# x^T's two parts at the front of their pool, laid out as k-tile, token tile, token

## The chip, the cores and the metric

The program runs on one core of a Trainium2 chip. Its time is the time on the device in microseconds (us). The kernel before took 1495.61 us, the median of three runs that went from 1495.11 to 1495.95.

## The reference

The reference is two transformer-like blocks on one sequence of 256 tokens with 1024 features, all in float32. The first is an FFN, a mixer (a causal convolution beside chunked gated linear attention), a second FFN and a gated projection. The second has two layers; each is an FFN, a mixing step (differential attention in the first layer, spatial gating in the second) and another FFN, and each part is scaled, shifted and gated by vectors made from a condition. Cut to what matters here:

```python
def _swiglu(x, w_in, w_out):
    gate, up = jnp.split(x @ w_in, 2, axis=-1)
    return (jax.nn.silu(gate) * up) @ w_out

def first_block(x, p, ...):
    h = x
    h = h + 0.5 * _swiglu(_rmsnorm(h, ffn1_norm), ffn1_w_in, ffn1_w_out)
    z = _rmsnorm(h, mix_norm) @ w_in            # convolution and linear attention from z
    h = h + jnp.concatenate([y_conv, y_gla], axis=-1) @ w_out
    h = h + 0.5 * _swiglu(_rmsnorm(h, ffn2_norm), ffn2_w_in, ffn2_w_out)
    gate = jax.nn.sigmoid(_rmsnorm(h, ple_norm) @ ple_w_gate)
    h = h + gate * (p @ ple_w_proj)
    return _rmsnorm(h, final_norm)

def second_block(x, c, ...):
    for i in range(2):
        h = modulate(rms_norm(x, ln_ffn1[i]), sh1, sc1)
        x = x + 0.5 * g1 * swiglu(h, ffn1_wg[i], ffn1_wu[i], ffn1_wd[i])
        h = modulate(rms_norm(x, ln_mix[i]), sh2, sc2)
        x = x + g2 * mix(h)                     # attention, then spatial gating
        h = modulate(rms_norm(x, ln_ffn2[i]), sh3, sc3)
        x = x + 0.5 * g3 * swiglu(h, ffn2_wg[i], ffn2_wu[i], ffn2_wd[i])
        x = rms_norm(x, ln_out[i])
    return x
```

Every `@` with a large weight multiplies the normalized activations of all 256 tokens by a weight of 1024 (or 2816) rows.

## The kernel before, in words

The 256 tokens are two token tiles of 128. Before each projection, `norm_T` normalizes a tile, transposes it on TensorE (line 571) and stores x^T, features on the partitions, in eight k-tiles of 128 features.

Float32 products are made from float32r parts: a value is a high part H and a low part L, and a product is three products, H·H, L·H and H·L. So x^T is held as `xh` and `xl` (lines 377 and 378, written by ScalarE's cast and VectorE's subtraction in `split`, lines 498 and 499), and each weight as `wh` and `wl` (lines 196 and 197). The weights come as a stream of 318 entries of 1 MB, three in flight, each split when there is room.

x^T is used in two ways. In `chunk`, with `mm3` (lines 490 to 492), 128 tokens of x^T for one k-tile are the weights that TensorE loads, and 512 columns of `wh` or `wl` are streamed. In `chunkT`, with `mmT` (line 692), 128 columns of `wh` or `wl` are loaded, and x^T of all 256 tokens for one k-tile is streamed: with the token tile as the outer index in `xh`, this is two pieces of 128 elements. An FFN takes its first two of eleven gate and up chunks by `chunk`, the other nine by `chunkT`; each of the nine is 8 k-tiles x 4 column blocks x 3 products = 96 products of line 692. Between two chunks come the down projection's products with `g` (128 tokens of the activated product, high and low) as weights, again by `mm3`. The other tiles whose names end in `HL` (`cHL` of the convolution, `oHL` of the attention) are weights of `mm3` too, and `wglr` is a small weight that line 692 loads in the mixer (tile `glr`).

The order of work is set by the program's order and by a scheduler with priorities; generators interleave the norms of one token tile with the products of the other. The pool `const` holds `h`, `kc`, `cols`, `neghalf`, `ones_r`, `xh`, `xl`, `cact` in the order in which `setup` asks for them, each rounded up to a multiple of 32 bytes in each partition.

Of the kernel before, what the change touches and what calls it, by code (L numbers as in the profile page):

```python
# [30 lines left out]
# buffers of each tag; tiles of one tag are handed out in the order of the program,  # L31
# so chains of work that run beside each other have tags of their own
# [6 lines left out]
# how many down-projection steps a tile does alone at the end of an FFN,  # L39
# and how many gate/up chunks the first tile does alone at its start  # L40
TAIL = 3
HEAD = 2
# taps of the convolution issued per us of the tensor engine's work
CONV_RATE = 3.0
# taps of each channel that the tensor engine takes
# [4 lines left out]
# how far ahead of its place in the program the scheduler may take a chain's work  # L50
# [6 lines left out]
# ---------------------------------------------------------------- weights  # L57
# Each entry of the stream is [128, 2048]: two blocks [128, 1024] of a weight.
#   "c": four k-tiles x 512 columns (two of each 1 MB entry make 8 k-tiles)
#   "d": two k-tiles x 1024 columns  # L60
#   "ada": transposed, two blocks of 128 columns of a modulation vector x 1024 rows
# [33 lines left out]
# the modulation vectors of the second block (shift, scale, gate of each part)  # L95
# are made while these FFNs run: layer, vectors
# [30 lines left out]
# columns of the packed per-partition constants  # L127
# [17 lines left out]
# columns of the shape-only constants  # L145
K_ID, K_LOW, K_UP, K_END, K_CAUSAL = 0, 128, 256, 384, 384
# rows
# [3 lines left out]
class Stream:  # L151
    """The weights, in order: DMA ahead, then split into H + L, float32r parts
    whose sum is the float32 weight."""
# [21 lines left out]
    def pump(self, now=False, n=0):  # L175
        """splits what there is room for, or n halves of an entry"""
# [38 lines left out]
class Task:  # L215
    """A chain of work given as a generator. What it yields is how much work of the
    tensor engine (us) is to be issued before the chain goes on, or a task to wait for."""
# [7 lines left out]
class Kernel:  # L225
# [25 lines left out]
    # -------------------------------------------------------------- order of issue  # L251
    @contextmanager
    def ahead(self, n):
        """the scheduler takes what is traced inside as if it were n instructions earlier"""
        tc = self.tc
        at = tc.cur_priority
        tc.cur_priority = at - n
        yield
        tc.cur_priority += n

    def pin(self, i):
        """what `after` is given later does not go before i on its engine"""
        self.pins[i.ins.engine] = i.ins
# [8 lines left out]
    def hold(self, on):  # L272
        """no weights are split while a chain runs that the tensor engine waits for"""
        self.held = on
        if not on:
            self.ws.pump()
# [31 lines left out]
    def tick(self, us):  # L308
        """so much work of the tensor engine has been issued"""
# [22 lines left out]
    # -------------------------------------------------------------- tiles  # L332
# [11 lines left out]
    def junk(self):  # L344
        """what only its sum is needed of"""
        return self.sp.tile([P, 512], BF16, tag="junk", name=self.nm("junk"), bufs=1)
# [7 lines left out]
    def psa(self, s, i, shape):  # L354
        """a bank of the accumulators, where none is in use"""
        return self.pacc.tile(shape, F32, tag=f"acc{i // 2}{i % 2}", name=self.nm(s))
# [10 lines left out]
    # -------------------------------------------------------------- start  # L367
    def setup(self):
        nc, a = self.nc, self.a
        self.h = [self.cpool.tile([P, D], F32, name=f"h{t}") for t in range(NT)]  # L370
# [4 lines left out]
        self.ones_r = self.cpool.tile([P, P], F32R, name="ones_r")  # L375
        nc.gpsimd.memset(self.ones_r.bitcast(F32), 1.0)
        self.xh = self.cpool.tile([P, NT, KT, P], F32R, name="xh")
        self.xl = self.cpool.tile([P, NT, KT, P], F32R, name="xl")
# [3 lines left out]
        # the first function of the scalar engine, of the table that the others here are in too  # L382
# [12 lines left out]
    def start(self):  # L395
        """x^T of the input, and the first weights"""
# [17 lines left out]
        # products of ones, that nothing reads, bring the tensor engine to its full clock  # L414
# [20 lines left out]
    # -------------------------------------------------------------- modulation  # L435
# [18 lines left out]
    def ada_end(self, layer, v, s):  # L454
        """a modulation vector: in columns, the gates in rows"""
# [30 lines left out]
    # -------------------------------------------------------------- pieces  # L486
# [8 lines left out]
    def split(self, dst, src):  # L495
        """dst = (H, L), src float32 in SBUF or PSUM"""
# [10 lines left out]
    def square(self, x, s):  # L507
        """sum of squares / 1024 of half a row"""
# [4 lines left out]
    def rstd(self, ss, t):  # L513
        """1/rms from the two halves' sums; with four, also that of 1/rms times what the other two are of"""
# [6 lines left out]
        if n == 2:  # L521
            # (s2 / (s1 + eps) + eps)^-1/2 (s1 + eps)^-1/2 = (s2 + eps (s1 + eps))^-1/2
# [6 lines left out]
    def residual(self, t, hf, gate, scale, keep):  # L529
        """h + gate * acc, half a row: in h, or keeps h"""  # L530
# [16 lines left out]
    def norm_T(self, t, ss, a, b=None):  # L547
        """x^T of tile t: (h / rms) * a + b, features on partitions, as H and L"""
# [40 lines left out]
        for hf in range(2):  # L589
            sl = slice(4 * hf, 4 * hf + 4)  # L590
            for i in self.split((self.xh[:, t, sl, :], self.xl[:, t, sl, :]), xas[hf]):
                if self.held:
                    self.pin(i)
            yield 0.5
# [5 lines left out]
    def xk(self, t, k):  # L600
        return self.xh[:, t, k, :], self.xl[:, t, k, :]
# [9 lines left out]
    def finish(self, t, scale=None, gate=None, a=None, b=None, row=None, upd=None, last=False):  # L611
        """h += ..., then the norms that lead to the next x^T"""
# [38 lines left out]
    # -------------------------------------------------------------- projections  # L651
    def chunk(self, key, t, ps):
        """ps[128 tokens, 512] = x @ chunk, over 8 k-tiles"""
# [8 lines left out]
    def by_tile(self, name, cs, pss=None):  # L662
        """several chunks, all of them for one token tile before the next"""
# [6 lines left out]
    def chunkT(self, key, banks):  # L670
        """the transpose of x @ chunk: 128 columns on the partitions, all tokens;
        bank [128, 2, 256] i of the two has column blocks i and i + 2"""
# [3 lines left out]
        for k in range(KT):  # L676
            h, l = self.ws.get((*key, k // 4), (k % 4) // 2)
            for cb in range(4):
# [3 lines left out]
                    (self.xh[:, :, k, :], self.xl[:, :, k, :]), k == 0 and cb < 2, k == KT - 1,  # L682
# [4 lines left out]
    def mmT(self, out, w, x, first, last):  # L687
        """out[columns, tokens] += w^T x; the groups of a bank share its first start"""
# [8 lines left out]
    def down(self, t, units, first, last):  # L697
        """acc[t] += x[k-tile]^T @ weight[k-tile] over units (key, half, x)"""
# [10 lines left out]
    def down2(self, name, order, xs, fin):  # L709
        """the product with a weight of four entries: the first token tile ends early enough  # L710
        for its norms to run beside the rest of the second's"""
# [14 lines left out]
    def ffn(self, name, fin):  # L726
# [39 lines left out]
        # first chunks: a token tile at a time, so that the first need not wait for the second  # L766
# [25 lines left out]
    # -------------------------------------------------------------- first block: mixer  # L792
    def mixer_load(self):
        nc, a = self.nc, self.a
        yield 30.0
        # the 16 columns of the gate's low rank, padded to the array's width
# [15 lines left out]
    def conv_taps(self, b):  # L812
        """depthwise causal convolution of a block of channels, a tap at a time"""
# [16 lines left out]
    def conv_diag(self):  # L830
        """diagonal matrices of the last taps, for each block of channels"""
# [9 lines left out]
    def conv_pe(self, bs):  # L841
        """the last taps of some blocks of channels, as products with diagonal matrices"""
# [41 lines left out]
    def gla_gates(self, zt):  # L884
        """decays of the gated linear attention, channels on the partitions"""
# [42 lines left out]
    def gla_scores(self, banks, gates):  # L928
        """q, k with their decays; scores inside the chunks of 64; k of the chunks' end by tokens"""
# [17 lines left out]
        for t in range(NT):  # L947
# [6 lines left out]
            for e in range(2):  # L954
                # a bank for each half of the array's rows
# [12 lines left out]
    def gla_state(self, c):  # L968
        """S_{c+1} = exp(cum_end) * S_c + k_end^T v"""
# [77 lines left out]
    def mixer(self, fin):  # L1047
# [4 lines left out]
        # a * sigmoid(b): the first half of the channels a token tile at a time  # L1052
# [33 lines left out]
        # low rank of the gates  # L1086
        pz = self.psg("glr", [P, S])
        for k in range(KT):
            self.mmT(
                pz, (self.wglr[0][:, k, :], self.wglr[1][:, k, :]), (self.xh[:, :, k, :], self.xl[:, :, k, :]),  # L1090
# [52 lines left out]
    # -------------------------------------------------------------- first block: per-layer embedding  # L1143
# [37 lines left out]
    # -------------------------------------------------------------- differential attention  # L1181
    def attn_load(self):
        """bias of each head by distance, and lambda"""
# [21 lines left out]
        # lambda_init + e0 - e1, negated  # L1205
# [8 lines left out]
    def attn_qk(self, c, t, ps):  # L1214
        """q or k of four heads: rms norm of the groups of 64, channels on the partitions"""
# [22 lines left out]
    def attn_softmax(self, hf, pr, t, lane):  # L1238
        """p0 - lambda * p1 of two heads, transposed"""
# [22 lines left out]
        for i in range(2):  # L1262
            # the bias is stored from the last key to the first
# [40 lines left out]
    def attn_values(self, hf, t, deps):  # L1304
# [12 lines left out]
        # squares scaled by 2^-40; a sum beyond float32's range gives 1/rms = 0  # L1317
# [62 lines left out]
    # -------------------------------------------------------------- spatial gating  # L1380
# [84 lines left out]
    # -------------------------------------------------------------- all of it  # L1465
# [57 lines left out]
# ---------------------------------------------------------------- host: layout only  # L1523
# [6 lines left out]
def pack(inputs):  # L1530
# [21 lines left out]
    def ch(dst, parts, half):  # L1552
        # parts: column blocks of a [1024, n] weight; four k-tiles of it
# [75 lines left out]
    # bucket of the distance n - 127  # L1629
# [38 lines left out]
```

## Time and profile before

| | |
|---|---|
| median of 3 runs | 1495.61 us (1495.11 to 1495.95) |
| span of the profiled execution | 1494.0 us |
| TensorE products (PE) | 1467.5 us busy, 98% |
| TensorE weight loads (PEld) | 1300.4 us, 87% |
| VectorE (DVE) | 1086.6 us, 73% |
| ScalarE (ACT) | 782.3 us, 52% |
| DMA | 232 GB/s in the mean |

The time of the profiled execution is given by its span, 1494.0 us from the first to the last instruction; the median of the runs is 1.6 us more, which lies around the span. Products on TensorE overlap: the record of a product is longer than the distance to the next one's start, so the duration in a row is no pace. A pace is the distance between two starts, or the length of a stretch divided by its products.

### The profile page before, as it was taken

The numbers are of one execution on the slowest core, as the hardware profiler recorded it, in microseconds if no ns is written. First come the engines' busy times: TensorE is split into PE (matmuls) and PEld (weight loads), VectorE is DVE, ScalarE is ACT, GpSimd is POOL, SyncE is SP. The second block draws the span as 40 slices with busy tenths as digits, with TensorE's granted clock in tenths as the row PEclk, the third lists the DMA queues.
The fourth block names the chain that finished last, engine by engine and source line by source line (L and its number), as shares of the span: only waits on it lengthen the run. The fifth ranks groups of instructions, "written<-read, shape, count | busy, mean of one in ns | idle before, by whom it ended". The sixth has DMA issues, their size and how long they took to land.

```text
span 1494.0 us, 23272 instructions
## 1 busy us (share of the span) xinstructions
PE 1467.5 (98%) x9256; PEld 1300.4 (87%) x9256; DVE 1086.6 (73%) x1693; ACT 782.3 (52%) x1238; POOL 55.2 (4%) x60
## 2 busy tenths in 40 slices
PE   8999999999999999999999999999999999999998
PEld 6999989779999878999776889998899988889997
DVE  6876569978775688775678788866987658685554
ACT  6544566265444584444586554446544455554442
POOL 1000000100000000000122100000000000000000
PEclk9999999999999999999999999999999999999999
DMA  8887544138776448786445388863899846276550
GB/s 311 335 310 267 191 149 183 64 134 319 296 290 233 148 157 320 301 315 216 155 141 199 116 330 347 325 249 127 312 350 335 300 145 235 105 291 225 205 204 29
DMA packets 52332, 346.06 MB, mean 232 GB/s; under 512 B 5912, under 2 KB 8704, under 8 KB 11776
## 3 DMA queue, kind: packets, MB, share of 16 engines
q1 hardware_dynamic: 52224, 344.58, 62.2%
q8 instruction: 72, 1.18, 0.3%
q14 instruction: 36, 0.29, 0.1%
HBM read 343.47 MB, written 1.09 MB: 231 GB/s over the span
## 4 chain that ended last, share of the span: by engine, by line
PE 80%; DVE 9%; ACT 4%; DMA 3%; issue 2%; POOL 2%; SPq 0%; POOLq 0%; DVEq 0%; ACTq 0%
PE gu L692 39%; PE acc L492 9%; PE acc L490 9%; PE acc L491 9%; DVE wl L197 4%; DMA raw<-wpack 3%; PE gu L491 2%; PE gu L492 2%; PE gu L490 2%; ACT wh L196 1%; DVE cacc L824 1%; PE xT L571 1%; POOL rn L504 1%; ACT s L1275 1%; PE cv L848 1%
## 5 line engine op out<-in xcount | busy, mean ns | idle before, releaser
L197 DVE TENSOR_TENSOR wl<-raw,wh 128x1024 fp32r<-128x1024 f32 x490 | 588.2, 1221 | 244.2 <-ACT wh L196 243.4
L196 ACT CAST wh<-raw 128x1024 fp32r<-128x1024 f32 x490 | 502.2, 1050 | 396.4 <-DMA raw<-wpack 159.4
L692 PE MATMUL gu<-xh,wh 128*128 128x256 f32 x1728 | 484.3, 281 | 1.8 <-DVE g L736 1.1
L692 PE MATMUL gu<-xl,wh 128*128 128x256 f32 x1728 | 482.2, 279 | 0.0
L692 PE MATMUL gu<-xh,wl 128*128 128x256 f32 x1728 | 482.1, 279 | 0.0
L692 PEld LDWEIGHTS gu<-xh,wh 128*128 128x128 f32 x1728 | 324.8, 188 | 5.1 <-DVE g L736 1.7
L692 PEld LDWEIGHTS gu<-xl,wh 128*128 128x128 f32 x1728 | 324.8, 188 | 2.4
L692 PEld LDWEIGHTS gu<-xh,wl 128*128 128x128 f32 x1728 | 324.8, 188 | 0.0
L492 PE MATMUL acc<-wl,g 128*128 128x512 f32 x528 | 207.2, 392 | 0.0
L490 PE MATMUL acc<-wh,g 128*128 128x512 f32 x528 | 207.2, 394 | 0.0
L491 PE MATMUL acc<-wh,g 128*128 128x512 f32 x528 | 206.5, 391 | 0.0
L447 DVE SCALAR_TENSOR_TENSOR raw<-raw,cact 128x1024 f32<-128x1024 f32 x144 | 171.7, 1219 | 17.9 <-DMA raw<-wpack 17.8
L492 PEld LDWEIGHTS acc<-wl,g 128*128 128x128 f32 x528 | 99.1, 188 | 22.4
L491 PEld LDWEIGHTS acc<-wh,g 128*128 128x128 f32 x528 | 99.1, 188 | 20.8 <-DVE g L499 1.2
L490 PEld LDWEIGHTS acc<-wh,g 128*128 128x128 f32 x528 | 99.2, 188 | 18.8
L734 ACT ACTIVATE s<-gu 128x256 f32<-128x256 f32 x108 | 40.7, 384 | 78.5 <-PE gu L692 78.3
L490 PE MATMUL gu<-wh,xh 128*128 128x512 f32 x192 | 76.7, 400 | 1.8 <-ACT wh L196 1.4
L492 PE MATMUL gu<-wl,xh 128*128 128x512 f32 x192 | 76.1, 398 | 1.4 <-DVE wl L197 1.4
L491 PE MATMUL gu<-wh,xl 128*128 128x512 f32 x192 | 76.3, 398 | 0.5 <-DVE xl L499 0.5
L736 DVE TENSOR_TENSOR g<-gu,s 128x256 f32<-128x256 f32 x108 | 44.6, 420 | 30.1 <-ACT s L734 29.5
L504 POOL TENSOR_TENSOR rn<-nv,neghalf 128x1 f32<-128x1 f32 (+1 forms) x22 | 20.1, 912 | 1244.6 <-DVE nv L518 1025.8
L498 ACT CAST g<-g 128x256 fp32r<-128x256 f32 x108 | 43.3, 407 | 38.1 <-DVE g L736 37.3
(308 smaller groups left out, 1623.6 us busy)
## 6 DMA issues: line engine op xcount, KB each, us to landing
raw<-wpack SPq DMA_DIRECT2D x316, 1024.0 KB, 4.9
gate<-grow SPq DMA_DIRECT2D x6, 512.0 KB, 4.2
row<-rows SPq DMA_DIRECT2D x5, 512.0 KB, 5.7
bias<-fd SPq DMA_DIRECT2D x16, 128.0 KB, 4.1
raw<-wpack SPq DMA_DIRECT2D x2, 512.0 KB, 7.1
out<-h SPq DMA_DIRECT2D x4, 256.0 KB, 2.2
h<-x SPq DMA_DIRECT2D x2, 256.0 KB
h<-x SPq DMA_DIRECT2D x1, 512.0 KB
```

The source lines that it names most:

```text
L196: self.last = k.after(nc.scalar.copy(out=h, in_=raw[:, u, :]))
L197: k.after(nc.vector.tensor_sub(out=l, in0=raw[:, u, :], in1=h.bitcast(F32)))
L447: self.after(nc.vector.scalar_tensor_tensor(out=raw[:, u, :], in0=raw[:, u, :], scalar=1.0, in1=self.cact, op0=ALU.mult, op1=ALU.mult, acc ...
L490: nc.tensor.matmul(out, lhsT=xh, rhs=wh, start=first, stop=False)
L491: nc.tensor.matmul(out, lhsT=xl, rhs=wh, start=False, stop=False)
L492: nc.tensor.matmul(out, lhsT=xh, rhs=wl, start=False, stop=last)
L498: self.nc.scalar.copy(out=dst[0], in_=src),
L504: self.nc.gpsimd.tensor_tensor(out=r, in0=v, in1=self.neghalf[:, :n], op=ALU.pow)
L571: self.last_T = nc.tensor.transpose(ps[:, i, :], xn[hf][:, i * P : (i + 1) * P], self.ident)
L692: nc.tensor.matmul(out, lhsT=ww, rhs=xx, start=first and n == 0, stop=last and n == 2, skip_group_check=True)
L734: nc.scalar.activation(s, b[:, 0, :], AF.Silu)
L736: nc.vector.tensor_mul(out=y, in0=b[:, 1, :], in1=s)
```

## The change

`xh`, `xl` and `ones_r` are asked for first in their pool, and the two parts of x^T change their layout from [token tile, k-tile, token] to [k-tile, token tile, token]. All that reads or writes them indexes accordingly. The rest of the difference between the two files is removed comments, which move later line numbers by one at most (line 692 becomes 693, lines 490 to 492 become 491 to 493).

```diff
     def setup(self):
         nc, a = self.nc, self.a
+
+        self.xh = self.cpool.tile([P, KT, NT, P], F32R, name="xh")
+        self.xl = self.cpool.tile([P, KT, NT, P], F32R, name="xl")
+        self.ones_r = self.cpool.tile([P, P], F32R, name="ones_r")
         self.h = [self.cpool.tile([P, D], F32, name=f"h{t}") for t in range(NT)]
...
-        self.ones_r = self.cpool.tile([P, P], F32R, name="ones_r")
         nc.gpsimd.memset(self.ones_r.bitcast(F32), 1.0)
-        self.xh = self.cpool.tile([P, NT, KT, P], F32R, name="xh")
-        self.xl = self.cpool.tile([P, NT, KT, P], F32R, name="xl")
...
-            for i in self.split((self.xh[:, t, sl, :], self.xl[:, t, sl, :]), xas[hf]):
+            for i in self.split((self.xh[:, sl, t, :], self.xl[:, sl, t, :]), xas[hf]):
...
     def xk(self, t, k):
-        return self.xh[:, t, k, :], self.xl[:, t, k, :]
+        return self.xh[:, k, t, :], self.xl[:, k, t, :]
...
-                    (self.xh[:, :, k, :], self.xl[:, :, k, :]), k == 0 and cb < 2, k == KT - 1,
+                    (self.xh[:, k, :, :], self.xl[:, k, :, :]), k == 0 and cb < 2, k == KT - 1,
...
-                pz, (self.wglr[0][:, k, :], self.wglr[1][:, k, :]), (self.xh[:, :, k, :], self.xl[:, :, k, :]),
+                pz, (self.wglr[0][:, k, :], self.wglr[1][:, k, :]), (self.xh[:, k, :, :], self.xl[:, k, :, :]),
```

In the built programs this gives the following addresses (byte in each partition, and what is left over 128):

| tile | before | after |
|---|---|---|
| `xh` | 118432 (32) | 106624 (0) |
| `xl` | 126624 (32) | 114816 (0) |
| `ones_r` | 117920 (32) | 123008 (0) |
| `wh`, `wl` | 41088 and on (0) | same |
| `g`, `oHL` | 169536 and on (64) | same |
| `wglr` | 185920, 206400 (64) | same |
| `cHL` | 139520 and on (0) | same |

`h`, `kc`, `cols` and `neghalf` move too, and each keeps its remainder, 0. The slices that a product takes of any of these tiles start at a multiple of 512 bytes from the tile's start. Streamed x^T of one k-tile was two pieces of 512 bytes, 4096 bytes apart, and is one of 1024 bytes; a write of half a k range of one token tile was one piece of 2048 bytes, and is four of 512 bytes, 1024 bytes apart. No instruction is added, removed or moved on any engine, and each waits for what it waited for.

## Rows read from the trace of the kernel before

**Rows 1.** The page: busy us of each engine, and clock by slices.

```profile
PE 1467.5 (98%) x9256; PEld 1300.4 (87%) x9256; DVE 1086.6 (73%) x1693; ACT 782.3 (52%) x1238; POOL 55.2 (4%) x60
PEclk9999999999999999999999999999999999999999
```

**Rows 2.** Chain that ended last: start us, us, what.

```profile
4.02 9.93 DMA raw<-wpack
22.55 7.44 DMA raw<-wpack
44.62 6.44 DMA raw<-wpack
72.28 11.21 PE gu L692 x96
...
462.32 11.20 PE gu L692 x96
...
1458.86 11.21 PE gu L692 x96
```

**Rows 3.** Timeline, first and last of 94: start us, us, engine line op.

```profile
1232.96 0.40 PE L492 MATMUL si<-wl,xh 128*128 128x512 f32 x1
...
1254.66 0.39 PE L492 MATMUL su<-wl,xh 128*128 128x512 f32 x1
```

**Rows 4.** Timeline, g as weights, first and last of 39.

```profile
493.61 0.39 PE L492 MATMUL acc<-wl,g 128*128 128x512 f32 x1
...
502.32 0.39 PE L492 MATMUL acc<-wl,g 128*128 128x512 f32 x1
```

**Rows 5.** Timeline, cHL as weights, first and last of 39.

```profile
307.94 0.39 PE L492 MATMUL acc<-wl,cHL 128*128 128x512 f32 x1
...
316.77 0.39 PE L492 MATMUL acc<-wl,cHL 128*128 128x512 f32 x1
```

**Rows 6.** Timeline, wglr as weights, first and last of 24.

```profile
225.31 0.28 PE L692 MATMUL glr<-xh,wglr 128*128 128x256 f32 x1
...
228.06 0.28 PE L692 MATMUL glr<-xh,wglr 128*128 128x256 f32 x1
```

**Rows 7.** Groups by form: line, names, xcount, busy us, mean ns, idle before.

```profile
L692 PE MATMUL gu<-xh,wh 128*128 128x256 f32 x1728 | 484.3, 281 | 1.8 <-DVE g L736 1.1 <-DVE g L775 0.7
L492 PE MATMUL acc<-wl,g 128*128 128x512 f32 x528 | 207.2, 392 | 0.0
L490 PE MATMUL gu<-wh,xh 128*128 128x512 f32 x192 | 76.7, 400 | 1.8 <-ACT wh L196 1.4 <-ACT xh L498 0.3
```

**Rows 8.** Timeline, 128-wide products in a row.

```profile
196.12 1.04 PE L571 MATMUL xT<-kc,xn 128*128 128x128 f32 x8
...
823.92 2.84 PE L1314 MATMUL o<-v,aT 128*128 128x128 f32 x24
```

**Rows 9.** Groups by form: the writes of x^T, and 128-wide operations.

```profile
L499 DVE TENSOR_TENSOR xl<-xa,xh 128x512 fp32r<-128x512 f32 x40 | 25.9, 685 | 5.7 <-ACT xh L498 5.7
L498 ACT CAST xh<-xa 128x512 fp32r<-128x512 f32 x40 | 23.3, 637 | 0.0
L580 ACT ACTIVATE xa<-xT,mod,mod 128x128 f32<-128x128 f32 x48 | 18.0, 456 | 4.7 <-PE xT L571 4.7
L584 DVE TENSOR_SCALAR xa<-xT,mod,mod 128x128 f32<-128x128 f32 x48 | 16.3, 402 | 0.2 <-PE xT L571 0.2
```

**Rows 10.** Waits of TensorE: us in total, times, longest.

```profile
PE gu L491 <- DVE xl L499: 0.5, 1, 0.5
PE gu L490 <- ACT xh L498: 0.3, 1, 0.3
```

**Rows 11.** Timeline, products (PE) and weight loads (PEld) side by side.

```profile
72.47 0.28 PE L692 MATMUL gu<-xh,wh 128*128 128x256 f32 x1
72.47 0.19 PEld L692 LDWEIGHTS gu<-xl,wh 128*128 128x128 f32 x1
72.59 0.28 PE L692 MATMUL gu<-xl,wh 128*128 128x256 f32 x1
```

## The prediction

> **What bounds the kernel now.** [...] Busy time of overlapping products hides their pace, so next I took the chain of waits. After the first 57 us, which hang on weight transfers and splits, it runs through block after block of 96 products of line 692 in 11.20 to 11.21 us [rows 2], with nothing between them. Start to start that is 11.21 / 96 = 116.8 ns. Everything that this change can give or cost lies in such paces: how far apart TensorE starts two neighbouring products. The built program has the same instructions in the same order on every engine, with the same waits, so nothing is issued earlier or later by rule; only where x^T lies and how it is stepped through is new.
>
> The third view is the timeline, for the pace of 512-wide products by what their weights are. With x^T as weights, 94 starts take 1254.66 - 1232.96 = 21.70 us, 233.3 ns each [rows 3]. With g as weights, 39 starts take 8.71 us, 229.2 ns [rows 4]. Both stream the same wh and wl (on multiples of 128 bytes), both at full clock, with no wait between. What differs is the address: g starts 64 past a multiple of 128, x^T 32 past one. A third kind, cHL, lies on a multiple of 128 and takes 8.83 us for 39 starts, 232.4 ns [rows 5]. So the pace does depend on address, by 1 to 4 ns. For 256-wide products there is one such pair: with wh or wl as weights (multiples of 128) 116.8 ns, with wglr (64 past) 24 starts in 2.75 us, 119.6 ns [rows 6], while the streamed x^T is the same.
>
> **The change part by part.**
>
> *x^T as weights, 512 wide.* The heads of the six FFNs have 192 such products on each of lines 490, 491 and 492 [rows 7], 576 in all; counted from the code, qkv, v, ab, r, si, su and the last product of the first block add 192, 144, 48, 48, 96, 96 and 96: 1296. Their address goes from 32 past a multiple of 64 to a multiple of 128. The ends are g's pace and cHL's: 233.3 - 229.2 = 4.1 ns gives -5.3 us, 233.3 - 232.4 = 0.9 ns gives -1.2 us. cHL is the nearer by address, g by far the better sampled (528 products per line, [rows 7]). I take the middle, 2.5 ns: -3.2 us. No 512-wide row in this trace is steadily slower than 233.3, so I put no loss here.
>
> *x^T streamed, 256 wide.* Line 692 has 1728 products of each of three kinds for gate and up [rows 7], 5184, and the code has 96 + 96 + 24 more for qk, ab and glr: 5400. Now each reads two pieces of 128, 4096 bytes apart, both starting 32 past a multiple of 64; afterwards one piece of 256 on a multiple of 128. No row shows an aligned, one-piece 256-wide product of this type, so I bound it. If time goes by column, an aligned one costs half of an aligned 512-wide one, 229.2 / 2 = 114.6 ns; with any fixed part it costs more. The upper end of a plain gain is today's 116.8. I take the middle, 115.7: -1.1 ns x 5400 = -5.9 us. Further ends, kept for the range: 128-wide float32 products, in which a load of 128 weight columns comes with only 128 streamed ones, start every (2.84 - 0.28) / 23 = 111.3 ns (o) and (1.04 - 0.28) / 7 = 109 ns (xT) [rows 8], which I take for the pace of the loads; and 119.6 of glr above.
>
> *The writes of x^T.* 40 casts on ScalarE and 40 subtractions on VectorE, 637 and 685 ns for 128x512 [rows 9], now write four pieces of 128 a kilobyte apart. Far end: each as dear as four separate 128-wide operations, 4 x 456 and 4 x 402 ns, so +1.2 and +0.9 us. TensorE waits for them once each in the whole span, 0.3 and 0.5 us [rows 10], because the other token tile's products cover them; if both waits took that full price it would be +2.1 us. The near end, the same lanes and element counts, is nothing, and I take nothing.
>
> *What of it reaches the end.* The blocks of line 692 follow each other without a gap, so a gain there passes on, except in the first 57 us, where the chain is DMA [rows 2]; about 4% of the 5400 lie there: -5.7 us. VectorE has to keep up with a faster TensorE; at 73% busy it can for a change below 1%. Of the 1296, those of the first head and about half of those in the attention stretch, where waits for VectorE and GpSimd lie between, are covered; I drop a fifth: -2.6 us. Sum: -8.3 us. The profiled execution has a span of 1494.0, 1.6 us below the median of the runs, 1495.6; the same stands around the new span. 1495.6 - 8.3 = 1487.3 us.
>
> [...] The 4.1 ns between [rows 3] and [rows 4] say that 32 bytes of offset matter. [...]
>
> **The rivals.**
>
> *The layout of what is streamed costs nothing, and the load paces line 692.* Each weight load starts beside the product before its own (72.47 both), and its own product starts 0.12 us later [rows 11]. If that time is the load's, no layout of x^T changes 5400 of the products. For it: the paces of 128-wide products are only 5 to 8 ns less. Against: those loads are as large, and take less. Then only the weights' part remains, by cHL's pace -1.2 us, or nothing at all: 1494.4 to 1495.6 us. [...]
>
> *The offset or the two pieces cost much more than I take.* Then line 692 falls to the load's pace: (116.8 - 111.3) or (116.8 - 109) x 5400 x 0.96 = -28.5 or -40 us, with the weights' -2.6: 1464 or 1453 us. For it: nothing in the trace shows the operand read well. Against: aligned one-piece 512-wide products are not that fast per column (114.6 for half).
> [...]
>
> *Slower: streamed operand and weights now lie alike.* In the new program wh, wl and x^T all start 128 past a multiple of 512. If the loads that run under a product disturb its stream, and how much depends on the distance of the two addresses, then 119.6 against 116.8 [rows 6, 2] and 232.4 against 229.2 are that effect: of the second pair the slower row, cHL over wh, has both on multiples of 128. Were 256-wide products to go to glr's pace, +2.8 ns x 5400 = +15.1 us, less 1.2: 1509.5 us. It decides from 116.8 + 0.5 ns on, where it eats the 2.6 us. Against it: of the three kinds of 512-wide products the equal one is not the worst; 233.3 of [rows 3] is, and there the two lie 32 apart.
> [...]
>
> **How the numbers follow.** Forecast 0.46, its own range 1481 to 1492.4; no effect but on weights, or none, 0.24; much more 0.14; slower 0.16. A measurement of this kernel tells about 0.2%, 3 us, from no change (three runs spread over 0.84 us). Faster: 0.45 of the forecast's and all of the third, 0.59. Same: the second, and small remnants of forecast and slower rival, 0.26. Slower: 0.15. The range reaches down to 1463, just below the nearer value of the third case, and up to 1500, a third of the slower rival's way, which leaves out half of the third and most of the fourth: 2 in 10.
>
> **What would show it.** In the new chain a block of 96 takes 11.1 us (115.7 ns) by the forecast, 11.2 by the first rival, 10.5 to 10.7 by the second, 11.4 to 11.5 by the third. The run of si and su shows the weights' part: at 230.8 ns its 94 starts take 21.46 us, against 21.70. Casts and subtractions of x^T over 700 ns, or waits for them of over 1 us, would prove the writes mispriced. The forecast is wrong if blocks of line 692 keep 11.2 us, or if they gain and the end of the span does not move.

## The result, and the profile after

The changed kernel took 1506.26 us (1505.15 to 1509.77, four runs) against 1495.68 of the kernel before (the three runs known at first and one more): a ratio of 1.0075, 95% interval 1.006 to 1.0089. It is slower, by about 11 us; the profiled execution's span went from 1494.0 to 1505.2 us. The forecast was 1487.3, and the range ended at 1500.

The page after, busy us of the engines and the granted clock, stands against [rows 1]:

```profile
PE 1477.6 (98%) x9256; PEld 1318.0 (88%) x9256; DVE 1087.6 (72%) x1693; ACT 781.2 (52%) x1238; POOL 55.3 (4%) x60
PEclk9999999999999999999999999999999999999999
```

The number of products is the same, yet TensorE is busy 10.1 us longer. VectorE and ScalarE have moved by about 1 us each. The granted clock was 0.997 in the mean where it was 0.999. One stretch of the attention, from 824 to 828 us, had 0.58 and 0.57 after, and from start to start 14 products there took 1.4 us more; from 60 to 800 us and from 1000 to 1400 us it was 1.00 after as before. So all but about 1.4 us went into the products at the clock of before. The chain of waits after (start us, us, what), to be held against [rows 2]:

```profile
56.05 11.74 PE gu L693 x96
71.22 11.52 PE gu L693 x96
88.25 11.50 PE gu L693 x96
...
1469.73 11.52 PE gu L693 x96
```

A block of 96 takes 11.50 to 11.52 us where it took 11.20 to 11.21: 119.9 ns from product to product, 3.1 more. That is all over the program, from the first FFN to the last. The other use of x^T went the other way. The timeline's first and last of the 94 products of [rows 3] are now:

```profile
1242.23 0.40 PE L493 MATMUL si<-wl,xh 128*128 128x512 f32 x1
...
1263.36 0.39 PE L493 MATMUL su<-wl,xh 128*128 128x512 f32 x1
```

They take 21.13 us instead of 21.70, 227.2 ns each against 233.3, faster than any 512-wide row before. The products with wglr as weights, 24 of them in [rows 6], went from 119.6 to (228.68 - 225.97) / 23 = 117.8 ns:

```profile
225.97 0.28 PE L693 MATMUL glr<-xh,wglr 128*128 128x256 f32 x1
...
228.68 0.28 PE L693 MATMUL glr<-xh,wglr 128*128 128x256 f32 x1
```

Both programs issue the same 9256 products in the same order, so the distance from each start to the next can be compared one by one. Added up over the two traces: +15.1 us behind the 5400 products that stream x^T, -3.7 us behind the 1296 that load it, -0.2 us behind all others; together +11.2, the difference of the spans. Of the 1296, those that the next product follows within 300 ns went from 233.3 to 228.1 ns in the mean, not to 227.2 everywhere; that is -6.3 us. Of this, 2.6 us came back as gaps of more than 300 ns, where TensorE waits for other engines. The waits of TensorE show a part of it (us in total, times, longest). Before:

```profile
PE xT L571 <- DVE xn L560: 3.1, 11, 0.5
PE qT L1231 <- DVE qn L1227: 2.3, 3, 1.0
```

After, where the wait for x^T itself is as in [rows 10]:

```profile
PE xT L572 <- DVE xn L561: 4.5, 11, 0.8
PE qT L1232 <- DVE qn L1228: 2.7, 3, 1.2
...
PE gu L491 <- ACT xh L499: 0.3, 1, 0.3
```

The writes of x^T in four pieces cost nothing. The groups after, against [rows 9], are 688 and 637 ns for 685 and 637:

```profile
L500 DVE TENSOR_TENSOR xl<-xa,xh 128x512 fp32r<-128x512 f32 x40 | 26.0, 688 | 5.7 <-ACT xh L499 5.6
L499 ACT CAST xh<-xa 128x512 fp32r<-128x512 f32 x40 | 23.3, 637 | 0.0
```

### The profile page after: what moved, and what is told of

Read it like the earlier page. It is cut to its first block, busy times and chain, and to the rows that moved or that the text cites. A ratio compares the mean times of both kernels' runs of the same rounds, so it can differ in the third digit from the quotient of the medians.

```text
span 1505.2 us, 23272 instructions
## 1 busy us (share of the span) xinstructions
PE 1477.6 (98%) x9256; PEld 1318.0 (88%) x9256; DVE 1087.6 (72%) x1693; ACT 781.2 (52%) x1238; POOL 55.3 (4%) x60
## 4 chain that ended last, share of the span: by engine, by line
PE 82%; DVE 9%; ACT 3%; issue 2%; POOL 2%; DMA 1%; SPq 0%; POOLq 0%; DVEq 0%; ACTq 0%
PE gu L693 41%; PE acc L493 9%; PE acc L492 9%; PE acc L491 9%; DVE wl L197 4%; PE gu L492 2%; PE gu L493 2%; PE gu L491 2%; DMA raw<-wpack 1%; PE xT L572 1%; ACT wh L196 1%; DVE cacc L825 1%; POOL rn L505 1%; ACT s L1276 1%; PE cv L849 1%
## 5 line engine op out<-in xcount | busy, mean ns | idle before, releaser
L693 PE MATMUL gu<-xh,wh 128*128 128x256 f32 x1728 | 491.4, 284 | 0.4 <-DVE g L776 0.4
L693 PE MATMUL gu<-xl,wh 128*128 128x256 f32 x1728 | 489.5, 283 | 0.0
L693 PE MATMUL gu<-xh,wl 128*128 128x256 f32 x1728 | 489.4, 283 | 0.0
L693 PEld LDWEIGHTS gu<-xh,wh 128*128 128x128 f32 x1728 | 329.1, 190 | 3.7 <-DVE g L776 1.0
L693 PEld LDWEIGHTS gu<-xl,wh 128*128 128x128 f32 x1728 | 329.1, 190 | 2.3
L693 PEld LDWEIGHTS gu<-xh,wl 128*128 128x128 f32 x1728 | 329.1, 190 | 0.0
```

Source lines behind the costliest of these rows:

```text
L693: nc.tensor.matmul(out, lhsT=ww, rhs=xx, start=first and n == 0, stop=last and n == 2, skip_group_check=True)
```

## The experiments

Two theories stood at the start. Theory D: the pace depends on the distance between the address that a product streams and the address from which the next product's weights are loaded, and not on the pieces. Theory L: reading x^T in one piece is what slowed the 256-wide products, and the addresses helped the others.

**The layout alone.** The new layout at the old addresses:

```diff
-        self.xh = self.cpool.tile([P, KT, NT, P], F32R, name="xh")
-        self.xl = self.cpool.tile([P, KT, NT, P], F32R, name="xl")
-        self.ones_r = self.cpool.tile([P, P], F32R, name="ones_r")
         self.h = ...
...
+        self.ones_r = self.cpool.tile([P, P], F32R, name="ones_r")
         nc.gpsimd.memset(self.ones_r.bitcast(F32), 1.0)
+        self.xh = self.cpool.tile([P, KT, NT, P], F32R, name="xh")
+        self.xl = self.cpool.tile([P, KT, NT, P], F32R, name="xl")
```

> x^T's parts get the new layout (k-tile, token tile, token) but keep their old addresses, 32 past a multiple of 128. Theory D (the pace of a product depends on the distance between the address that is streamed and the address from which the next weights are loaded, not on the pieces): 256-wide products stay at 116.7 ns, products with x^T as weights at 233.3 ns, time as before, 1495.6 us. Theory L (reading x^T in one piece is what makes the 256-wide product slower): 256-wide at 120.0 ns, weights at 233.3 ns, time 1495.6 + 5400 x 3.3 ns = 1513 us.

Measured: 1495.45 us, ratio 0.9998 (0.9988 to 1.0007). Its chain, as above:

```profile
72.06 11.20 PE gu L693 x96
88.77 11.21 PE gu L693 x96
```

The blocks are those of before to the hundredth, 11.20 to 11.21 us with one piece and with two. The pieces make no difference here, and the writes in four pieces cost nothing that shows in the time.

**The addresses alone.** The new addresses with the old layout:

```diff
-        self.xh = self.cpool.tile([P, KT, NT, P], F32R, name="xh")
-        self.xl = self.cpool.tile([P, KT, NT, P], F32R, name="xl")
+        self.xh = self.cpool.tile([P, NT, KT, P], F32R, name="xh")
+        self.xl = self.cpool.tile([P, NT, KT, P], F32R, name="xl")
```

(with the old indices in the four places that use them).

> x^T's parts get the new addresses, multiples of 128, but keep the old layout, so a 256-wide product streams two pieces. Theory D: 256-wide products at 120.0 ns and products with x^T as weights at 226.7 ns, as with the whole change, time 1506 us. Theory L: 256-wide at 116.7 ns, weights at 226.7 ns, time 1495.6 - 1296 x 6.6 ns = 1487 us.

Measured: 1505.31 us, ratio 1.0068 (1.0053 to 1.0083): the whole loss. The chain shows blocks as after the change:

```profile
71.83 11.52 PE gu L693 x96
88.86 11.50 PE gu L693 x96
```

Theory L falls. What is left is the address.

**A map of distances.** A kernel in which only TensorE works:

```diff
+    for kind in ("one", "two", "wide"):
+        for m in range(4):                 # streamed operand 32 m bytes past a multiple of 512
+            for v in range(16):            # weights 32 v bytes past a multiple of 512
+                ps = pp.tile([P, n], F32, name=f"{kind}_{'abcd'[m]}_{'abcdefghijklmnop'[v]}")
+                for _ in range(24):
+                    nc.tensor.matmul(ps, lhsT=w[:, 8 * v : 8 * v + 128], rhs=rhs, start=True, stop=True)
```

> Only TensorE works: 24 products in a row for each of 3 x 4 x 16 cases, nothing of the reference is computed. Streamed operand of 256 columns in one piece, 256 in two pieces 4096 bytes apart, or 512; it starts 0, 32, 64 or 96 bytes (a to d) past a multiple of 512, the weights 0 to 480 bytes in steps of 32 (a to p). Theory D: the pace depends on the difference of the two, alike for one and two pieces; with difference 0 it is 120.0 and 226.7 ns, at weights 32 below the streamed 116.7 ns (256 wide), at weights 32 above 233.3 ns (512 wide), at 64 below 229 ns (512 wide). Theory L: two pieces are faster than one by some 3 ns at every offset, and the pace hangs on each operand's own offset from a multiple of 64. If neither offset nor pieces matter without the other engines' traffic, all of a kind are equal.

Some stretches of its timeline (start us, us, ..., xcount). A stretch lasts 23 paces and one product's own 0.28 us, or 0.39 when 512 wide:

```profile
13.84 3.03 PE L47 MATMUL one_a_a<-x,w 128*128 128x256 f32 x24
16.71 3.00 PE L47 MATMUL one_a_b<-x,w 128*128 128x256 f32 x24
...
59.31 2.96 PE L47 MATMUL one_b_a<-x,w 128*128 128x256 f32 x24
...
195.64 3.04 PE L47 MATMUL two_a_a<-x,w 128*128 128x256 f32 x24
...
241.12 2.96 PE L47 MATMUL two_b_a<-x,w 128*128 128x256 f32 x24
...
377.45 5.62 PE L47 MATMUL wide_a_a<-x,w 128*128 128x512 f32 x24
382.91 5.75 PE L47 MATMUL wide_a_b<-x,w 128*128 128x512 f32 x24
...
410.91 5.67 PE L47 MATMUL wide_a_g<-x,w 128*128 128x512 f32 x24
```

One piece and two agree (3.03 and 3.04, 2.96 and 2.96). In ns, the mean of the last 12 distances between starts of a stretch (the first can run at another pace: all 23 of wide_a_a come to (5.62 - 0.39) / 23 = 227.4 ns, the last 12 to 226.7), by weights' address minus streamed address, for a streamed operand on a multiple of 512:

| distance, bytes | 0 | 32 | 64 | 96 | 128 | 160 | 192 | 224 |
|---|---|---|---|---|---|---|---|---|
| 256 columns | 120.0 | 118.2 | 117.8 | 117.1 | 118.3 | 120.0 | 117.8 | 117.8 |
| 512 columns | 226.7 | 233.3 | 233.3 | 234.3 | 233.3 | 233.3 | 228.9 | 233.3 |

From 256 on the values repeat (24 products take 3.03 us at 0 and at 256, 5.62 and 5.61 when 512 wide), and moving the streamed operand by 32, 64 or 96 shifts the row by as much, with one exception: at distance -32 (the same as 224) with 256 columns, 116.7 ns came as well as 117.8. With no other engine at work these are the paces of the kernels. Before the change, x^T lay 32 above the weights modulo 256: loaded under a stream of wh at 32, 233.3; streamed over a load of wh at -32, 116.7. After: 0 both ways, 226.7 and 120.0. g stands at -64 (192): 228.9. wglr under x^T stood at -96 (160), 120.0, and now at -64, 117.8. So far theory D holds, with a period of 256 bytes. Every product of a stretch loads the same weights, so the map does not tell the distance to the next product's weights from that to the product's own.

**The same kernel 32 bytes further on.** One small tile moved in front:

```diff
+        self.neghalf = self.cpool.tile([P, 8], F32, name="neghalf")
         self.xh = self.cpool.tile([P, KT, NT, P], F32R, name="xh")
...
-        self.neghalf = self.cpool.tile([P, 8], F32, name="neghalf")
```

> The changed kernel with one small tile (neghalf, 32 bytes) moved in front of x^T's parts: they stay at the front of the pool and in the new layout, but start 32 past a multiple of 128, as far from the weights (modulo 256) as before the change. Theory D (distance of the two addresses modulo 256): 256-wide products back at 116.7 ns, x^T as weights at 233.3 ns, time 1495.5 us. Rival P (the place at the front of the pool, next to the weights, or the one-piece layout on aligned addresses makes the loss): 120 ns and about 1506 us remain, or a value between.

Measured: 1495.28 us, ratio 1.0002 (0.9993 to 1.0011), blocks of 11.21 us:

```profile
72.09 11.21 PE gu L693 x96
```

Rival P falls: neither the place at the front of the pool nor the layout makes the loss. 32 bytes do, with 1495.28 us against 1506.26.

**g at the weights' remainder.** The kernel before, with a pad:

```diff
         self.sp = E(tc.tile_pool(name="s", bufs=1))
+        self.sp.tile([P, 16], F32, tag="pad", name="pad", bufs=1)
```

> The kernel before, with a pad of 64 bytes at the start of the pool in which g lies, so that g, oHL, sHL and yHL start at the same remainder modulo 256 as the streamed weights. Theory D: products with these as weights go from 229.0 to 226.7 ns, 1824 x 2.1 ns = -3.8 us, cHL's 48 from 232 to 229; x^T untouched; time about 1491.5 us. Rival W (what such products save is eaten by the waits behind them, as half of it was for x^T as weights): paces as above, time within 1.5 us of before.

Measured: 1491.84 us, ratio 0.9986 (0.9977 to 0.9995). The distances behind g and the tiles like it sum to 2.4 us less, those behind the 256-wide products to 1.7 less, mostly shorter waits. The second sum is not the pad's: the layout alone and the kernel 32 bytes further on, with the old paces, have 1.4 and 1.8 us less there too. The timeline, first and last of the 39 of [rows 4]:

```profile
492.34 0.40 PE L493 MATMUL acc<-wl,g 128*128 128x512 f32 x1
...
501.02 0.39 PE L493 MATMUL acc<-wl,g 128*128 128x512 f32 x1
```

This stretch gained only 8.71 - 8.68 us, since its first ten distances are 224 to 240 ns before it settles at 226.7; over the whole program the commonest pace over six products of this kind is 226.7 ns where it was 228.8. The theory's pace came true, and 2.4 of its 3.8 us. Rival W, a time within 1.5 us of before, is not ruled out: the interval runs from 0.7 to 3.4 us less.

**A finer map.** As the map above, with weights at 0 to 252 bytes in steps of 4 and 48 products each:

```diff
-        for m in range(4):
-            for v in range(16):
+            for v in range(64):
...
-                for _ in range(24):
-                    nc.tensor.matmul(ps, lhsT=w[:, 8 * v : 8 * v + 128], rhs=rhs, start=True, stop=True)
+                for _ in range(48):
+                    nc.tensor.matmul(ps, lhsT=w[:, v : v + 128], rhs=x[:, 0:n], start=True, stop=True)
```

> Only TensorE works, nothing of the reference is computed: 48 products in a row for each distance of 0 to 252 bytes in steps of 4 between streamed operand (256 or 512 columns, at a multiple of 512) and weights. Theory D in its simplest form (what counts is in which stretch of 32 bytes a load begins): steps at multiples of 32, plateaus between, with the values of the 32-byte map; lowest 226.7 at 512 columns, about 117 at 256. Rival F (finer: 16 bytes, or each 4): values between two multiples of 32 that stand outside those of their neighbours.

Its timeline for distances 0, 28, 32, 52 and 64, 256 columns:

```profile
15.02 5.91 PE L39 MATMUL one_a_a<-x,w 128*128 128x256 f32 x48
54.91 6.57 PE L39 MATMUL one_a_h<-x,w 128*128 128x256 f32 x48
61.30 6.57 PE L39 MATMUL one_b_a<-x,w 128*128 128x256 f32 x48
91.12 5.63 PE L39 MATMUL one_b_f<-x,w 128*128 128x256 f32 x48
107.99 5.61 PE L39 MATMUL one_c_a<-x,w 128*128 128x256 f32 x48
```

There are no plateaus, so theory D in its simplest form falls, and rival F holds: in one stretch of 32 bytes (5.91 - 0.28) / 47 = 119.8 ns at 0 and (6.57 - 0.30) / 47 = 133.4 at 28 (the last product there takes 0.30 us; by the starts themselves it is 133.3), in the next 133.3 at 32 and 113.8 at 52. And two distances differ from the first map: 32 (133.3 against 118.2) and 64 (113.4 against 117.8). At 32 the stretch before ran at 133.3 too. Theory K was formed here: the products settle on one of several paces, and which one hangs on what ran before.

**x^T 64, 76 and 52 bytes before the weights.** In the changed kernel, x^T's parts as views into one larger tile, from element 48, 45 or 51 on (and one buffer fewer of a tiny tile, for room):

```diff
-        self.xh = self.cpool.tile([P, KT, NT, P], F32R, name="xh")
-        self.xl = self.cpool.tile([P, KT, NT, P], F32R, name="xl")
+        xb = self.cpool.tile([P, 2 * KT * NT * P + 64], F32R, name="x")
+        self.xh, self.xl = (
+            xb[:, at : at + KT * NT * P].rearrange("p (k t n) -> p k t n", k=KT, t=NT)
+            for at in (48, 48 + KT * NT * P)
+        )
...
-        st = self.tiny(f"st{t}", 12)
+        st = self.tiny(f"st{t}", 12, 1)
```

> The changed kernel with x^T 64 bytes before the weights modulo 256: under a 256-wide product the next weights are loaded from 64 further on, under a 512-wide one x^T from 64 before. The two maps differ on this distance: 117.8 ns over 24 products in the first, 113.3 ns over 48 in the second. Theory D with a pace that locks (Theory K: products with a small weight load in their shadow settle on one of a few paces, and which one hangs on the pace before): either 113.3 ns, then 1495.5 - 5400 x 3.4 ns = 1477 and some 3 less by x^T as weights at 228.8 ns, about 1474 us; or 117.8 ns, then about 1498 us. Plain theory D of the first map: 1498 us.

> As before, x^T 76 bytes before the weights modulo 256, not a multiple of 32. By the map in steps of 4 bytes, 256-wide products at 113.3 ns and x^T as weights at 233 ns: 1495.5 - 18.4 = 1477 us. Rival: the traffic of the other engines, which the map lacked, breaks the pace of 113.3 ns; 117 to 120 ns, 1497 to 1513 us.

> As before, x^T 52 bytes before the weights modulo 256. By the map in steps of 4 bytes, 256-wide products at 113.3 ns after a few at 114 to 120, x^T as weights at 235 ns: about 1479 us. Rival: traffic breaks the pace; 117 to 120 ns, 1498 to 1515 us.

Measured: 1479.30 us at 64 (ratio 0.9898, 0.9883 to 0.9913), 1511.92 at 76 (1.0116, 1.0101 to 1.0131), 1499.17 at 52 (1.0025, 1.0014 to 1.0037). The chains, one kernel each. At a distance of 64:

```profile
72.21 10.91 PE gu L696 x96
88.61 10.91 PE gu L696 x96
```

At 76:

```profile
72.05 11.52 PE gu L696 x96
```

At 52:

```profile
71.94 11.25 PE gu L696 x96
```

At 64 the blocks fall to 113.6 ns, the pace of the finer map, and the kernel takes 1.0% less than the one before and 1.8% less than the changed one. At 76 and 52 the finer map's 113.3 did not come: 120.0 and 117.2. In the kernel it is the streamed operand that lies off a multiple of 32, in the map it was the weights, and the other engines are at work; whether either of the two is the reason was not tried. At distances of 0, 32 and 192 the kernels show the paces of the first map; at 64 and 224 they took one of the two that the maps give; at 76 and 52 the map did not carry over.

**Both gains together.** The kernel at 64 with the pad for g:

```diff
         self.sp = E(tc.tile_pool(name="s", bufs=1))
+        self.sp.tile([P, 16], F32, tag="pad", name="pad", bufs=1)
```

> The kernel with x^T 64 bytes before the weights (1479.3 us) and the pad of 64 bytes that puts g, oHL, sHL and yHL at the weights' remainder modulo 256. If the two gains are independent: 256-wide products at 113.4 ns, g at 226.7 ns, 1479.3 - 3.5 = 1475.8 us. Theory K (a pace locks, and which one hangs on what ran before): behind products at 226.7 instead of 229.0 ns the 256-wide ones may settle at 117.8 ns instead, and the time would be about 1475.8 + 5000 x 4.4 ns = 1498 us.

Measured: 1491.66 us, ratio 0.9976 (0.9967 to 0.9985): 12 us slower than without the pad. The chain:

```profile
73.46 11.31 PE gu L697 x96
90.21 11.31 PE gu L697 x96
```

11.31 us is 117.8 ns. x^T and its weights lie where they lay at 10.91, and the products between the blocks run at another pace. That fits theory K, though the time is 6 us below its 1498. The run does not show it alone: the pad moved every tile of that pool by 64 bytes, also those that ScalarE and VectorE read and write. The next experiment has TensorE alone.

**The same distance behind different products.**

```diff
+    before = {"p": (512, 0), "q": (512, 48), "r": (256, 7), "s": (256, 32)}   # columns, distance / 4
+    for v in range(8):
+        d = "abcdefgh"[v]
+        for b, (n, at) in before.items():
+            run(f"pre_{b}_{d}", n, at, 24)
+            run(f"one_{b}_{d}", 256, 8 * v, 96)
```

> Only TensorE works, nothing of the reference is computed: 96 products of 256 columns for each distance of 0 to 224 bytes in steps of 32 (last letter a to h), each time behind 24 products of four kinds (p: 512 wide at distance 0, q: 512 wide at 192, r: 256 wide at 28, s: 256 wide at 128). Theory K: some distances, 64 among them, show two paces by what ran before (113.3 or 117.8 at 64, 116.7 or 117.8 at 224), 0 always 120.0. Without locking: one pace for each distance, whatever ran before.

The timeline at distance 64 (c), behind each of the four, and one stretch each of distances 0 (a) and 160 (f):

```profile
19.41 11.68 PE L37 MATMUL one_p_a<-x,w 128*128 128x256 f32 x96
...
144.14 11.47 PE L37 MATMUL one_p_c<-x,w 128*128 128x256 f32 x96
160.95 11.47 PE L37 MATMUL one_q_c<-x,w 128*128 128x256 f32 x96
175.06 11.47 PE L37 MATMUL one_r_c<-x,w 128*128 128x256 f32 x96
...
189.21 11.06 PE L37 MATMUL one_s_c<-x,w 128*128 128x256 f32 x96
...
330.45 11.67 PE L37 MATMUL one_p_f<-x,w 128*128 128x256 f32 x96
```

Three stretches of distance 64 at 117.8 and one at 113.5 ns, for the same 96 products; the one at 113.5 writes the same one of the program's four buffers in PSUM as the one behind q, which ran at 117.8. So the pace depends on what ran before, as theory K says. These stretches are of one execution; the kernel at 64 repeats its pace, with four runs between 1479.21 and 1479.43 us. Distance 96 showed 117.3, 118.7 and 120.0, distance 192 117.8 and 113.3, distance 224 116.7 and 117.8. Distances 0 and 160 were at 120.0 every time, and nothing here was slower: the change had put x^T on one of the two worst of these eight. Which pace follows is not known: behind 512-wide products at 192 (q) distance 64 ran at 117.8 here, while the kernel's blocks at 64, most of them behind g at 192, ran at 113.6.

**Shorter loads.** The map once more, with weights of 128, 64 and 32 columns:

```diff
+        for c, cols in (("full", 128), ("half", 64), ("quarter", 32)):
+            for v in range(8):
...
+                for _ in range(48):
+                    nc.tensor.matmul(ps[0:cols, :], lhsT=w[:, 8 * v : 8 * v + cols], rhs=x[:, 0:n], start=True, stop=True)
```

> Only TensorE works, nothing of the reference is computed: 48 products in a row, 256 (one) or 512 (wide) columns streamed from a multiple of 512, weights of 128 (full), 64 (half) or 32 (quarter) columns, at distances of 0 to 224 bytes in steps of 32 (a to h). Theory S (the load of the next weights, running under a product, holds up the stream, by how much depends on the distance): what depends on distance shrinks with the load, to half and a quarter, and the pace goes towards a floor that is the same at all distances, near 109 ns at 256 columns (the pace of xT). Rival O (the distance acts otherwise, at the start of each product): the differences between distances stay as they are with full loads, 6 to 8 ns at 512 columns.

At 256 columns:

```profile
14.54 5.91 PE L39 MATMUL one_full_a<-x,w 128*128 128x256 f32 x48
...
60.01 5.62 PE L39 MATMUL one_half_a<-x,w 128*64 128x256 f32 x48
71.08 5.86 PE L39 MATMUL one_half_c<-x,w 128*64 128x256 f32 x48
...
104.89 5.82 PE L39 MATMUL one_quarter_a<-x,w 128*32 128x256 f32 x48
116.18 5.62 PE L39 MATMUL one_quarter_c<-x,w 128*32 128x256 f32 x48
```

With the full load the paces of the eight distances lie between 117.4 and 119.9 ns in this run. With half a load they go from 113.6 (distance 0) to 118.7 (64 and 224), with a quarter from 113.3 (96) to 117.9 (0); at 512 columns with a quarter from 230.6 to 239.1. The spread does not shrink with the load, and no floor near 109 appears, so theory S falls as stated. Rival O does not hold either: which distance is the slow one changes with the load's length. What exactly a load does to the stream beside it stays open.

## Why the prediction was wrong

- *What bounds the kernel.* Right: the time followed the pace of the products, and the span grew by the 11.2 us that the distances between starts grew by.
- *x^T streamed, 256 wide.* This is the step that failed: -5.9 us as forecast, +15.1 us measured. I took half of the aligned 512-wide product as the lower end, today's pace as the upper, and the middle. That assumes that an aligned operand read in one piece can only help. The layout alone and the kernel 32 bytes further on read one piece and keep the 11.20 to 11.21 us a block of before, so the pieces are no term here. Nor is alignment at multiples of 32 bytes: in the map 24 products at distance 0 take 3.03 us with both operands on multiples of 512 and with both 32 past one. The distance to the loaded weights is the term, and it went from 224 to 0, from 116.7 to 120.0 ns. The lower end did not hold either: at a distance of 64 the blocks ran at 113.6 ns, below 114.6.
- *x^T as weights, 512 wide.* The sign was right; that the net of -3.7 us lay near my -2.6 is luck, since two errors cancel. The paces were read by the wrong key. I sorted them by each operand's remainder over 128, so that cHL looked like the nearest row for the new x^T; its distance is 128, at which the map has 233.3. The new distance is 0, for which the map has 226.7, below both of my ends; in the kernel the mean pace came to 228.1, and 2.6 us went into waits.
- *The writes of x^T and the reach of the gain.* Nothing, as taken, and as the layout alone confirms. A fifth of the weights' part was dropped for cover. At 6.6 ns the 1296 would have saved 8.6 us, and 3.7 were left.
- *The third rival* named what happened: streamed operand and weights lying alike, glr's pace, 1509.5 us. It was given 0.16. What I held against it was that the equal pair, cHL over wh, was not the slowest 512-wide row; but that pair was not equal modulo 256. And 512-wide rows say nothing of 256-wide ones: in the first map distance 0 is the best of the eight for the one (226.7 ns) and, with 160, the worst for the other (120.0). Its price was right by chance: glr's products did not lie alike but at 160, which happens to have the pace of 0, 120.0 ns.

## What to carry to other kernels

When TensorE streams float32r products back to back, measure the pace from start to start, and treat the distance modulo 256 between what is streamed and what is loaded next as a parameter to be tried on the chip; a distance of 64 bytes gave 1% here and one of 0 bytes cost 0.7%. Maps made in isolation named the kernel's pace at 0, 32 and 192 bytes and left two paces open at 64 and 224. The pace also hung on the products that ran before (113.5 or 117.8 ns at 64 bytes, and 1479.30 us at 64 alone against 1491.66 with the pad for g), so two such gains must be measured together. Where no row shows the case in question, a "plain improvement" has a loss as its other bound.

## What the runs showed of the hardware

- Back-to-back float32r products of 256 columns with a load of 128 columns each run at 113.3 to 133.3 ns, by addresses and by what ran before, with a granted clock of 1.000 throughout the maps; of 512 columns, at 226.7 to 234.3 ns in the first map.
- In the first map the dependence repeats every 256 bytes (24 products of 256 columns take 3.03 us at a distance of 0 and of 256), and one piece or two pieces of the streamed operand made no difference (3.03 and 3.04 us, 2.96 and 2.96).
- Some paces recur: 113.3, 116.7, 120.0, 133.3, 226.7 and 233.3 ns are whole multiples of 3.33 ns, which is 120.0 / 36 (34, 35, 36, 40, 68 and 70 of it); 117.8 and 228.9 are not. At a distance of 64 bytes, 96 equal products ran at 113.5 or 117.8 ns by what came before them.
